# Layer 1's experts: 64 tokens gathered two experts per fetch, 192 dense, the last 64 with both coefficient halves in one stationary

## The chip, the cores and the metric

The kernel runs on one core of a Trainium2 chip. The metric is the device time of one execution in microseconds. A core has engines that run side by side, each with its own queue in order: TensorE (PE; the loads of its stationary operand are listed as PEld), VectorE (DVE), ScalarE (ACT), GpSimd (POOL), and SyncE (SP), whose queue here issues most transfers. Sixteen DMA engines move the data.

## The reference

Two layers, each a mixer and then an expert network (PEER) of 16,384 experts. Layer 0 runs the experts for 512 tokens (256 latent, 256 context), layer 1 for the 256 latent ones. For every token and each of eight heads a query is scored against two sets of 128 keys; the 16 best of each set are combined into 256 candidates, and the 16 best of those name experts.

```
s = einsum('thpd,hpkd->thpk', q, sub_keys)
sv, si = top_k(s, 16)
cand = sv[..., 0, :, None] + sv[..., 1, None, :]
cidx = si[..., 0, :, None] * 128 + si[..., 1, None, :]
best, pos = top_k(cand, 16)
eidx, gate = take_along_axis(cidx, pos), softmax(best)
ue, ve = take(u, eidx), take(v, eidx)          # rows of 1024
act = gelu(einsum('td,thkd->thk', x, ue)) * gate
ff = einsum('thk,thkd->td', act, ve)
```

So each token uses 128 of the experts, a row of u and one of v each.

## The kernel before

There are two ways to compute ff. **Dense:** all 16,384 experts are gone through in 128 blocks of 128, for all dense tokens at once: first half x times u, gelu, multiply by a matrix of gates (zero where an expert was not chosen), second half times v. **Gathered:** for 128 rows, an indirect DMA fetches for each row one chosen expert's u and v (8 KB); DVE takes the dot product with the row's token and adds v times the gated result. Layer 0 gathers for 128 tokens and is dense for 384; layer 1 is dense for all 256.

Float32 matmuls are split: an operand is written as a high part (`..h`, by ACT, rounded to float32r) and a low part (`..l`, the rest, by DVE or POOL), and `mm3` (lines 109 to 111) sums three float32r products.

Layer 1's expert network is `peer(1, ...)`, in these stages. *Choosing* (`evaluate`, `select`): PE makes a head's queries and scores, DVE the top 16. In between, `spare` computes the first half of some blocks ahead and puts them into DRAM (the stash): 32 of 128 blocks in layer 1, two of each eight. *Gates* (`dense`, lines 754 to 784): one-hot matmuls build the gate matrix G in units of 32 tokens; each unit is followed by two stashed blocks. `spare(len(waits))` computes those still missing. *The loop* (lines 922 on) runs over 128 blocks in an order written out by hand: each engine gets its instructions as the code lists them.

One pass of the loop, for block n: loads are issued (gates, v, u); PE makes the first half of block n+3 (24 matmuls, unless stashed) and ACT its gelu (`act`, line 735); for block n+1 DVE multiplies by the gates (line 903), ACT writes the high part `ch` (line 65), DVE the low part `cl` (line 73); for block n+5 ACT writes `uh` (line 719) and DVE `ul` (line 720), unless stashed; PE runs the second half of block n (`second`); for block n+2 ACT writes `vh` (line 880), DVE `vl` (line 881). In layer 0 a gather step follows, spread by `spent`: a piece of the next head's pick (DVE), `accum` for fetch e-3 (line 827, DVE), `fetch` e (line 811, POOL), `dot` for fetch e-2 (line 817, DVE), and on ACT a gelu and a scale of one column each (lines 818, 819).

Stashed blocks have no first half in the loop and no `uh` and `ul`. Raw u and v tiles come through a ring of five buffers. At the end the sums leave PSUM, are transposed and added to the stream (`combine`).

Of the kernel before, what the change touches and what calls it, by code (L numbers as in the profile page):

```python
# [9 lines left out]
F32 = mybir.dt.float32  # L10
F32R = mybir.dt.float32r
# [26 lines left out]
class Kern:  # L38
# [83 lines left out]
    def setup(self):  # L122
# [9 lines left out]
        make_identity(nc, self.ident)  # L132
        self.o1024 = c([128, 128])
# [362 lines left out]
    def peer(self, l, halves, gtile, nstash=0, nq=2, ng=(1, 1)):  # L496
# [3 lines left out]
        nt = 2 * len(halves)  # L500
        N = 128 * nt
        t0 = 1 if gtile else 0
        nd = nt - t0
        D0, ND = 128 * t0, 128 * nd
        with ExitStack() as st:
            m = self.open(st, f"p{l}")
            hh, hl = m([128, 8, N], F32R), m([128, 8, N], F32R)
            GA = m([128, nd, 128])
            IX = m([128, nd, 2, 128])
            iob = m([128, 16], BF16)  # L510
            nc.vector.tensor_copy(iob, self.iota[:, 0:16])
# [102 lines left out]
            with ExitStack() as st2:  # L614
# [8 lines left out]
                if gtile:  # L623
                    for g in range(2):
                        p = self.mm([128, 4, 128])
                        for k in range(4):
                            for n, x in enumerate((hh, hl)):
                                nc.tensor.matmul(p[:, k], x.bitcast(F32)[:, 4 * g + k, 0:128], self.ident, start=n == 0, stop=n == 1)
                        nc.scalar.activation(htok[:, g * 512:(g + 1) * 512].rearrange("p (k d) -> p k d", k=4), p, AF.Copy)
                keys = mq([128, 16, 128])  # L630
                nc.sync.dma_start(keys, i[f"keys{l}"])
                def evaluate(hd, w):

                    sv = mq([128, nd, 2, 16], F32, tag="sv", bufs=2)
                    si = mq([128, nd, 2, 16], U32, tag="si", bufs=2)
                    SC = []
                    for half in range(2):
# [8 lines left out]
                        sp = px([128, nt, 128], F32, tag="sp", bufs=2)  # L646
                        for t in range(nt):
                            nc.tensor.matmul(sp[:, t], qt[:, t * 128:(t + 1) * 128], keys[:, hp], start=True, stop=True)
                        sc = mq([128, nd, 128], F32, tag="sc", bufs=4)
                        nc.scalar.activation(sc, sp[:, t0:], AF.Copy)  # L650
                        if gtile:
                            nc.scalar.activation(scg[:, hp], sp[:, 0], AF.Copy)
                        SC.append(sc)
                    return hd, SC, sv, si

                def select(hd, SC, sv, si):
                    for half in range(2):
                        for t in range(nd):
                            topk(SC[half][:, t], sv[:, t, half], si[:, t, half], mq)
                    hs = slice(16 * hd, 16 * hd + 16)  # L660
                    choose(nd, sv, si, GA[:, :, hs], IX[:, :, :, hs], mq)

                with self.region():
                    prev = None
                    for b in range(4):
# [11 lines left out]
                    softmax(GA.rearrange("p t (h k) -> p (t h) k", k=16), 8 * nd, mq)  # L677
                    spare(nq)
            self.dense(l, t0, nd, hh[:, :, D0:], hl[:, :, D0:], IX, GA, first, stash, waits, spare, ng,
                       (htok, EI, gGA, scg, dacc, topk_parts, choose_parts, softmax) if gtile else None)  # L680

    def combine(self, l, tiles, halves, tmp, done=lambda k0: None):

        nc = self.nc
        for gq in range(2):
            for t, ff in tiles:
                hf = halves[t // 2]
                p = self.mm([128, 4, 128])
                for k in range(4):
                    nc.tensor.transpose(p[:, k], ff[:, (4 * gq + k) * 128:(4 * gq + k) * 128 + 128], self.ident)  # L690
                for k in range(4):
                    kk = 4 * gq + k
                    dst = self.s[hf][:, kk, (t % 2) * 128:(t % 2) * 128 + 128]
                    g = self.mt[l][:, 40 + kk, hf:hf + 1]
                    if k % 2:
                        x = tmp([128, 128], F32, tag="cmb", bufs=2)
# [43 lines left out]
    def dense(self, l, t0, nd, hh, hl, IX, GA, first, stash, waits, spare, ng, gather):  # L740
        nc, i = self.nc, self.i
        ND = 128 * nd
        halves = (0, 1) if l == 0 else (1,)
        with ExitStack() as st:
# [4 lines left out]
            with ExitStack() as st2:  # L749
                gb = self.open(st2, f"gb{l}")  # L750
                px = self.open(st2, f"gb{l}ps", space=PSUM)
                for t in range(nd):
                    tr = self.mm([128, 3, 128])
                    for n, x in enumerate((IX[:, t, 0], IX[:, t, 1], GA[:, t])):
                        nc.tensor.transpose(tr[:, n], x, self.ident)
                    trs = gb([128, 3, 128], F32, tag="trs", bufs=2)
                    nc.scalar.activation(trs, tr, AF.Copy)  # L757
                    for u in range(4):
# [473 lines left out]
```

## Time and profile before

| | us |
|---|---|
| runs: median of 3 | 2807.66 (2806.81 to 2807.99) |
| the profiled execution | 2807.95 |
| its span | 2806.2 |
| PE busy over the span | 2673.5 (95%) |
| DVE busy | 2028.2 (72%) |
| ACT busy | 1412.6 (50%) |
| POOL busy | 572.8 (20%) |

The span is what lies between the first and the last instruction of the program. PE's busy time is made of records whose ends are modelled and which overlap, so the rate of PE is read from starts. Start times below are microseconds from the span's start. A group by form keeps operand shapes apart.

### The profile page before, as it was taken

How to read it: one execution, taken by the hardware profiler on the slowest of the kernel's cores; microseconds unless marked ns; L12 is line 12 of the kernel's file. 1: busy time of each engine (PE TensorE's matmuls, PEld its weight loads, DVE VectorE, ACT ScalarE, POOL GpSimd, SP SyncE). 2: the span in 40 equal slices, each digit the busy share in tenths (PEclk: the TensorE clock that was granted, in tenths of full speed). 3: DMA queues.
4: the chain of work that ended last, by engine and by line, in shares of the span. 5: the costliest groups of instructions: out<-in, count | busy, mean ns of one | idle time of the engine just before them, and what ended most of it. 6: DMA issues, size and time to landing. Idle time of an engine off the chain costs nothing.

```text
span 2806.2 us, 40422 instructions
## 1 busy us (share of the span) xinstructions
PE 2673.5 (95%) x15043; PEld 2305.6 (82%) x15043; DVE 2028.2 (72%) x4323; ACT 1412.6 (50%) x2528; POOL 572.8 (20%) x538
## 2 busy tenths in 40 slices
PE   7999999999999999999999998998889999999998
PEld 4677778798988888898898896657789888888887
DVE  4688559999677787787878776656987655555555
ACT  5756543399444344444344436444388444444444
POOL 0000023288122222221222221005366000000000
PEclk9999999999999999999999999999999999999999
DMA  6334223445788878887778782354346665666653
GB/s 257 126 135 149 91 79 147 150 195 225 271 296 300 302 272 300 299 303 280 283 289 313 298 298 77 120 216 148 124 184 253 240 220 212 226 233 220 218 216 126
DMA packets 155204, 609.68 MB, mean 217 GB/s; under 512 B 10752, under 2 KB 90368, under 8 KB 90880
## 3 DMA queue, kind: packets, MB, share of 16 engines
q1 hardware_dynamic: 136576, 472.87, 46.0%
q0 software_dynamic: 18432, 134.23, 13.1%
q8 instruction: 119, 1.95, 0.3%
q14 instruction: 77, 0.63, 0.1%
HBM read 555.94 MB, written 51.12 MB: 216 GB/s over the span
## 4 chain that ended last, share of the span: by engine, by line
PE 47%; issue 22%; DVE 13%; POOL 12%; ACT 3%; DMA 1%; POOLq 0%; DVEq 0%; ACTq 0%
POOL uv L811 6%; POOL o L778 6%; PE t L109 6%; PE t L111 6%; PE t L110 6%; PE mm L111 5%; PE mm L109 5%; PE mm L110 5%; PE pj L111 2%; PE pj L109 2%; PE pj L110 2%; PE gp L780 2%; PE mm L168 1%; DVE eq L568 1%; PE pj L1065 1%
## 5 line engine op out<-in xcount | busy, mean ns | idle before, releaser
L109 PE MATMUL mm<-t,uh 128*128 128x384 f32 (+1 forms) x2048 | 637.1, 311 | 5.6 <-ACT c L735 3.0
L111 PE MATMUL mm<-t,ul 128*128 128x384 f32 (+1 forms) x2048 | 636.6, 311 | 2.2 <-POOL ul L720 2.2
L110 PE MATMUL mm<-t,uh 128*128 128x384 f32 (+1 forms) x2048 | 635.4, 310 | 0.1
L109 PE MATMUL t<-vh,ch 128*128 128x512 f32 x1280 | 502.4, 392 | 21.1 <-ACT ch L65 21.1
L111 PE MATMUL t<-vh,cl 128*128 128x512 f32 x1280 | 503.7, 394 | 0.0
L110 PE MATMUL t<-vl,ch 128*128 128x512 f32 x1280 | 501.6, 392 | 0.0
L109 PEld LDWEIGHTS mm<-t,uh 128*128 128x128 f32 x2048 | 387.0, 189 | 15.2 <-ACT c L735 3.7
L110 PEld LDWEIGHTS mm<-t,uh 128*128 128x128 f32 x2048 | 387.2, 189 | 9.2 <-DVE t L214 0.3
L111 PEld LDWEIGHTS mm<-t,ul 128*128 128x128 f32 x2048 | 387.2, 189 | 3.1 <-POOL ul L720 3.0
L720 DVE TENSOR_TENSOR ul<-r,uh 128x1024 fp32r<-128x1024 f32 x229 | 280.4, 1225 | 132.6 <-ACT uh L719 132.2
L811 POOL DMA_INDIRECT uv<-in_uv_dram,t x128 | 211.4, 1651 | 763.2 <-DVE t L827 715.8
L881 DVE TENSOR_TENSOR vl<-r,vh 128x1024 fp32r<-128x1024 f32 x256 | 312.6, 1221 | 73.3 <-PE t L110 51.0
L73 DVE TENSOR_TENSOR cl<-c,ch 128x384 fp32r<-128x384 f32 (+1 forms) x256 | 125.9, 492 | 308.0 <-ACT ch L65 308.0
L818 ACT ACTIVATE act<-act 128x1 f32<-128x1 f32 x128 | 26.0, 203 | 546.5 <-DVE uv L817 546.5
L109 PEld LDWEIGHTS t<-vh,ch 128*128 128x128 f32 x1280 | 241.4, 189 | 70.9 <-ACT ch L65 27.4
L719 ACT ACTIVATE uh<-r 128x1024 fp32r<-128x1024 f32 x256 | 270.4, 1056 | 52.3 <-PE mm L110 26.1
L111 PEld LDWEIGHTS t<-vh,cl 128*128 128x128 f32 x1280 | 241.0, 188 | 56.0 <-DVE cl L73 5.0
L110 PEld LDWEIGHTS t<-vl,ch 128*128 128x128 f32 x1280 | 240.9, 188 | 44.1
L880 ACT ACTIVATE vh<-r 128x1024 fp32r<-128x1024 f32 x256 | 268.8, 1050 | 0.0
L735 ACT ACTIVATE c<-mm 128x384 f32<-128x384 f32 (+1 forms) x256 | 110.7, 433 | 281.7 <-PE mm L111 280.4
L778 POOL TENSOR_SCALAR o<-t,trs 128x128 f32<-128x128 f32 x320 | 215.8, 693 | 52.8 <-ACT trs L757 45.8
L779 DVE TENSOR_SCALAR o<-t,trs 128x128 f32<-128x128 f32 x640 | 184.8, 362 | 0.0
(323 smaller groups left out, 4513.2 us busy)
## 6 DMA issues: line engine op xcount, KB each, us to landing
r<-in_ut_dram SPq DMA_DIRECT2D x128, 1024.0 KB
r<-in_vv_dram SPq DMA_DIRECT2D x128, 1024.0 KB
r<-in_wm_dram SPq DMA_DIRECT2D x48, 1024.0 KB
t<-buf SPq DMA_DIRECT2D x20, 2048.0 KB
gates<-t SPq DMA_DIRECT2D x32, 768.0 KB
r<-in_wq_dram SPq DMA_DIRECT2D x16, 1024.0 KB
gates<-t SPq DMA_DIRECT2D x16, 1024.0 KB
r<-in_ew_dram SPq DMA_DIRECT2D x14, 1024.0 KB
```

Source lines behind the costliest of these rows:

```text
L73: e[1].tensor_tensor(lo, x, hi.bitcast(F32), op=ALU.subtract)
L109: mm(p, a[0], b[0], start=first, stop=False)
L110: mm(p, a[0], b[1], start=False, stop=False)
L111: mm(p, a[1], b[0], start=False, stop=last)
L719: nc.scalar.activation(uh, t[:, x], AF.Copy)
L720: (eng or nc.vector).tensor_tensor(ul, t[:, x], uh.bitcast(F32), op=ALU.subtract)
L735: nc.scalar.activation(a, p, AF.Gelu_apprx_tanh)
L778: nc.gpsimd.tensor_scalar(o1, self.iota, trs[:, 0, tk:tk + 1], None, op0=ALU.is_equal)
L779: nc.vector.tensor_scalar(o2, self.iota, trs[:, 1, tk:tk + 1], trs[:, 2, tk:tk + 1], op0=ALU.is_equal, op1=ALU.mult)
L811: nc.gpsimd.indirect_dma_start(out=UV[e], out_offset=None, in_=i[f"uv{l}"], in_offset=bass.IndirectOffsetOnAxis(ap=EI[:, e:e + 1], axis=0))
L880: nc.scalar.activation(vh, v, AF.Copy)
L881: nc.vector.tensor_tensor(vl, v, vh.bitcast(F32), op=ALU.subtract)
```

## The change

In layer 1 the first 64 tokens go the gathered way. A fetch has 128 rows; row r and row r + 64 are the same token with different heads (0 to 3 and 4 to 7), so 64 fetches of two experts per token replace the dense work for these tokens. Their scores are put on both halves of the partitions (`scg`), their sums of both halves are added by a matmul with `halves` in `combine`. 192 tokens stay dense. The last 64 of these are scored the same way (`scb`: heads 0 to 3 in the upper half of the partitions, 4 to 7 in the lower), so heads 0 to 3 choose for one tile of 128 rows and heads 4 to 7 for two; the blocks of heads run in the order 0, 2, 1, 3. In the second half the high and low coefficients of these 64 tokens lie side by side in one stationary of 128 columns, against `vh` and `vl`: two matmuls for 64 tokens in place of three, and their pairs of rows are added by `pairs`. The coefficients are therefore stored as pairs (high, low), and the other tile's stationary is read with a step of two. The gate matrix has six units instead of eight. Layer 0 goes through the same code with its old sizes.

```diff
 def setup(self):
+        self.halves, self.pairs = c([128, 64]), c([128, 64])
+        nc.vector.tensor_add(self.halves, self.ident[:, 0:64], self.ident[:, 64:128])
+        nc.vector.tensor_add(self.pairs, self.ident[:, 0::2], self.ident[:, 1::2])
...
 def peer
+        ND = N - D0
+        nd, part64 = ND // 128, ND % 128 // 64
+        two = D0 == 64
+        W = 128 * nd + 64 * part64
+        NS = 64 if two else 128
...
+                for g in range(2):
+                    p = self.mm([128, 4, 128])
+                    for k in range(4):
+                        for o in (0, 64) if two else (0,):
                             for n, x in enumerate((hh, hl)):
+                                nc.tensor.matmul(p[o:o + D0, k], x.bitcast(F32)[:, 4 * g + k, 0:D0], self.ident, start=n == 0, stop=n == 1)
...
 def evaluate
+                        for t in range(nd):
+                            nc.tensor.matmul(sp[:, t], qt[:, D0 + t * 128:D0 + (t + 1) * 128], keys[:, hp], start=True, stop=True)
...
+                        rows, j = (slice(64 * (hd // 4), 64 * (hd // 4) + 64), hp % 8) if two else (slice(0, 128), hp)
+                        nc.tensor.matmul(sp[rows, 3], qt[:, 0:D0], keys[:, hp], start=True, stop=True)
+                        if two:
+                            nc.tensor.matmul(sp[rows, 2], qt[:, N - 64:N], keys[:, hp], start=True, stop=True)
+                            nc.scalar.activation(scb[rows, j], sp[rows, 2], AF.Copy)
+                        nc.scalar.activation(scg[rows, j], sp[rows, 3], AF.Copy)
+                        SC.append([sc[:, t] for t in range(nd)] + [scb[:, j] for _ in range(n - nd)])
...
-                    for b in range(4):
+                    for b in (0, 2, 1, 3) if two else range(4):
...
 def combine
+                    if rows is None:
+                        nc.tensor.transpose(p[:, k], x, self.ident)
+                    else:
+                        nc.tensor.matmul(p[:, k], x, rows, start=True, stop=True)
...
 def dense
-                for t in range(nd):
+                for t in range(nd + two):
+                    nk = min(128, ND - 128 * t)
...
-                    for u in range(4):
+                    for u in range(nk // 32):
...
-            if gather:
...
-                for e in range(131):
+            for e in range(NS + 3):
...
-            out = [[px([128, 512]) for _ in range(2)] for _ in range(nd)]
+            out = [[px([128, 512]) for _ in range(2)] for _ in range(nd + two)]
...
             def second(n, c, v):
+                if two:
+                    for x in range(2):
+                        xs = slice(x * 512, x * 512 + 512)
+                        mm = nc.tensor.matmul
+                        a, b = out[nd][x], c[:, 128:192].rearrange("p t y -> p (t y)")
+                        mm(a, b, v[0][:, xs], start=n == 0, stop=False)
+                        mm(a, b, v[1][:, xs], start=False, stop=n == 127)
+                    c = c[:, 0:128, 0], c[:, 0:128, 1]
+                    for x in range(2):
+                        xs = slice(x * 512, x * 512 + 512)
+                        self.mm3(out[0][x], c, (v[0][:, xs], v[1][:, xs]), n == 0, n == 127)
+                    return
...
             def gated(n):
+                    if two:
+                        S[n] = b2([128, ND, 2], F32R, tag="ch", bufs=2)
+                        self.split(c, S[n][:, :, 0], S[n][:, :, 1])
+                        return
...
-        self.peer(1, (1,), False, nstash=32, nq=6, ng=(2, 2))
+        self.peer(1, (1,), 64, nstash=32, nq=6, ng=(2, 2))
...
-    r["uv0"] = np.concatenate([d["p_u"][0], d["p_v"][0]], axis=1)
+    for l in range(2):
+        r[f"uv{l}"] = np.concatenate([d["p_u"][l], d["p_v"][l]], axis=1)
```

In the loop, DVE's queue before, two blocks (line 903 multiplies by the gates, 73 is the low part of the coefficients, 720 and 881 the low parts of u and v):

```order
L903 TENSOR_TENSOR c_21527<-c_21527,gates_21257 128x256
L73 TENSOR_TENSOR cl_21608<-c_21527,ch_21607 128x256
L720 TENSOR_TENSOR ul_21612<-r_21554,uh_21611 128x1024
L881 TENSOR_TENSOR vl_21628<-r_21448,vh_21627 128x1024
L903 TENSOR_TENSOR c_21581<-c_21581,gates_21257 128x256
L73 TENSOR_TENSOR cl_21639<-c_21581,ch_21638 128x256
L720 TENSOR_TENSOR ul_21643<-r_21554,uh_21642 128x1024
L881 TENSOR_TENSOR vl_21659<-r_21552,vh_21658 128x1024
L903 TENSOR_TENSOR c_21550<-c_21550,gates_21257 128x256
```

and after, two blocks (the same instructions at lines 945, 73, 744 and 911; 527 to 529 are a piece of a pick, 857 accumulates, 847 is the dot):

```order
L945 TENSOR_TENSOR c_20584<-c_20584,gates_20322 128x192
L73 TENSOR_TENSOR ch_20736<-c_20584,ch_20736 128x192
L744 TENSOR_TENSOR ul_20740<-r_20622,uh_20739 128x1024
L911 TENSOR_TENSOR vl_20754<-r_20620,vh_20753 128x1024
L527 MATCH_REPLACE s_20757<-sv_20527,t_16970 128x128
L528 MAX sv_20527<-s_20757 128x8
L529 MAX_INDEX si_20528<-sv_20527,s_20757 128x8
L857 SCALAR_TENSOR_TENSOR t_16971<-uv_20531,act_20651,t_16971 128x1024
L847 SCALAR_TENSOR_TENSOR uv_20612,act_20764<-uv_20612,t_16967 128x1024
L945 TENSOR_TENSOR c_20680<-c_20680,gates_20618 128x192
L73 TENSOR_TENSOR ch_20796<-c_20680,ch_20796 128x192
L744 TENSOR_TENSOR ul_20800<-r_20706,uh_20799 128x1024
```

Between a block's `vl` and the next block's multiply now stand a piece of a pick, an accumulate and a dot.

ACT's queue before, in the same loop (735 the gelu of the first half, 65 the high part, 719 and 880 the high parts of u and v):

```order
L880 ACTIVATE vh_21658<-r_21552 128x1024
L735 ACTIVATE c_21687<-mm_21662 128x256
L65 ACTIVATE ch_21690<-c_21550 128x256
L719 ACTIVATE uh_21694<-r_21635 128x1024
L880 ACTIVATE vh_21710<-r_21552 128x1024
L735 ACTIVATE c_21743<-mm_21718 128x256
```

and after (759, 65, 743 and 910 are these, 848 and 849 the gelu and the scale of a dot):

```order
L759 ACTIVATE c_21234<-mm_21209 128x192
L65 ACTIVATE ch_21237<-c_21134 128x192
L743 ACTIVATE uh_21240<-r_21107 128x1024
L910 ACTIVATE vh_21254<-r_21105 128x1024
L848 ACTIVATE act_21271<-act_21271 128x1
L849 ACTIVATE act_21271<-act_21271,t_16969 128x1
L759 ACTIVATE c_21300<-mm_21275 128x192
L65 ACTIVATE ch_21303<-c_21183 128x192
```

The two small instructions stand ahead of the next block's first-half gelu and high part.

PE's second half of a block before:

```order
L109 MATMUL t_20572<-vh_23262,ch_23294 128x512
L110 MATMUL t_20572<-vl_23263,ch_23294 128x512
L111 MATMUL t_20572<-vh_23262,cl_23295 128x512
L109 MATMUL t_20573<-vh_23262,ch_23294 128x512
L110 MATMUL t_20573<-vl_23263,ch_23294 128x512
L111 MATMUL t_20573<-vh_23262,cl_23295 128x512
L109 MATMUL t_20574<-vh_23262,ch_23294 128x512
L110 MATMUL t_20574<-vl_23263,ch_23294 128x512
L111 MATMUL t_20574<-vh_23262,cl_23295 128x512
L109 MATMUL t_20575<-vh_23262,ch_23294 128x512
L110 MATMUL t_20575<-vl_23263,ch_23294 128x512
L111 MATMUL t_20575<-vh_23262,cl_23295 128x512
```

and after (920 and 921 are the matmuls of the packed 64 tokens):

```order
L920 MATMUL t_20304<-vh_25343,ch_25375 128x512
L921 MATMUL t_20304<-vl_25344,ch_25375 128x512
L920 MATMUL t_20305<-vh_25343,ch_25375 128x512
L921 MATMUL t_20305<-vl_25344,ch_25375 128x512
L109 MATMUL t_20302<-vh_25343,ch_25375 128x512
L110 MATMUL t_20302<-vl_25344,ch_25375 128x512
L111 MATMUL t_20302<-vh_25343,ch_25375 128x512
L109 MATMUL t_20303<-vh_25343,ch_25375 128x512
L110 MATMUL t_20303<-vl_25344,ch_25375 128x512
L111 MATMUL t_20303<-vh_25343,ch_25375 128x512
```

Ten matmuls of 512 columns stand where twelve did.

## Rows read from the trace of the kernel before

**Rows 1.** Windows: us; busy PE, PEld, DVE, ACT, POOL; clock, DMA share, GB/s

```profile
717.00:1697.00 980.00, 960.11 (x4774) 860.54 (x4774) 760.65 (x1163) 401.04 (x740) 211.56 (x129) 1.00 0.79 291
1923.00:2046.00 123.00, 96.78 (x719) 93.16 (x719) 115.89 (x487) 44.52 (x72) 54.77 (x23) 0.89 0.37 131
2046.00:2165.00 119.00, 114.14 (x912) 110.68 (x912) 100.81 (x288) 109.20 (x226) 88.75 (x129) 0.98 0.58 220
2181.00:2797.00 616.00, 615.37 (x3758) 550.66 (x3756) 356.91 (x476) 288.43 (x440) 0.00 (x0) 1.00 0.59 214
```

**Rows 2.** Timeline, DVE, layer 1's loop: start, duration, instruction, idle before

```profile
2295.88 1.22 DVE L720 TENSOR_TENSOR ul<-r,uh 128x1024 fp32r<-128x1024 f32 x1 [0.53 <-ACT uh L719]
2297.03 1.22 DVE L881 TENSOR_TENSOR vl<-r,vh 128x1024 fp32r<-128x1024 f32 x1
2298.16 0.42 DVE L903 TENSOR_TENSOR c<-c,gates 128x256 f32<-128x256 f32 x1
2300.54 0.43 DVE L73 TENSOR_TENSOR cl<-c,ch 128x256 fp32r<-128x256 f32 x1 [1.96 <-ACT ch L65]
```

**Rows 3.** Timeline, ACT, the same stretch

```profile
2299.82 0.38 ACT L735 ACTIVATE c<-mm 128x256 f32<-128x256 f32 x1 [3.02 <-PE mm L111]
2300.10 0.41 ACT L65 ACTIVATE ch<-c 128x256 fp32r<-128x256 f32 x1
2300.40 1.05 ACT L719 ACTIVATE uh<-r 128x1024 fp32r<-128x1024 f32 x1
```

**Rows 4.** Timeline, PE, the same stretch

```profile
2302.16 0.39 PE L111 MATMUL t<-vh,cl 128*128 128x512 f32 x1
2302.39 0.28 PE L109 MATMUL mm<-t,uh 128*128 128x256 f32 x1
...
2305.22 0.40 PE L109 MATMUL t<-vh,ch 128*128 128x512 f32 x1
```

**Rows 5.** Timeline, PE, layer 1's mixer: passes of two columns

```profile
1876.20 0.95 PE L177 MATMUL mm<-t,modm 128*128 128x2 f32 x8
1877.01 0.36 PE L110 MATMUL pj<-l,whi 128*128 128x256 f32 x1
1877.21 0.28 PE L109 MATMUL pj<-h,whi 128*128 128x256 f32 x1
```

**Rows 6.** Timeline, DVE, layer 0's loop: accumulate and dot

```profile
1205.19 1.26 DVE L827 SCALAR_TENSOR_TENSOR t<-uv,act,t 128x1024 f32<-128x1024 f32 x1
1206.37 1.22 DVE L817 SCALAR_TENSOR_TENSOR uv<-uv,t 128x1024 f32<-128x1024 f32 x1
```

**Rows 7.** Timeline, ACT, layer 0's loop, behind that dot

```profile
1207.63 0.20 ACT L818 ACTIVATE act<-act 128x1 f32<-128x1 f32 x1 [4.42 <-DVE uv L817]
1207.87 0.29 ACT L819 ACTIVATE act<-act,t 128x1 f32<-128x1 f32 x1
1208.07 0.47 ACT L735 ACTIVATE c<-mm 128x384 f32<-128x384 f32 x1
1208.44 0.51 ACT L65 ACTIVATE ch<-c 128x384 fp32r<-128x384 f32 x1
1208.85 1.05 ACT L719 ACTIVATE uh<-r 128x1024 fp32r<-128x1024 f32 x1
```

**Rows 8.** Groups by form, DVE, the multiply by the gates

```profile
L903 DVE TENSOR_TENSOR c<-c,gates 128x384 f32<-128x384 f32 x128 | 71.0, 555 | 0.0
...
L903 DVE TENSOR_TENSOR c<-c,gates 128x256 f32<-128x256 f32 x128 | 53.6, 419 | 0.0
```

**Rows 9.** Timeline, ACT, stashed blocks with little else on the engines

```profile
2017.19 0.37 ACT L735 ACTIVATE c<-mm 128x256 f32<-128x256 f32 x1
...
2030.07 0.36 ACT L735 ACTIVATE c<-mm 128x256 f32<-128x256 f32 x1
```

**Rows 10.** The tile uv: an idle time of DVE before it, and landings

```profile
  DMA uv<-in_uv_dram,t: 0.5, 1
...
DMA to landing us min/median/max: 5.5/6.6/11.9
```

More of the change, by code (lines that the diff above doesn't have):

```diff
@@ L738, in first_half, with dense @@
         return load, part, dots, act, hold
-    def dense(self, l, t0, nd, hh, hl, IX, GA, first, stash, waits, spare, ng, gather):
+    def dense(self, l, D0, nd, ND, hh, hl, IX, GA, first, stash, waits, spare, ng, gather):
         nc, i = self.nc, self.i
-        ND = 128 * nd
+        two = ND > 128 * nd
         halves = (0, 1) if l == 0 else (1,)
@@ new lines, in dense, with pick @@
+            htok, EI, gGA, scg, dacc, topk_parts, choose_parts, softmax = gather
+            NS = EI.shape[1]
+            gp = self.open(st, f"gp{l}")
+            def pick(hd):
+                sv = gp([128, 1, 2, 16], F32, tag="sv", bufs=2)
+                si = gp([128, 1, 2, 16], U32, tag="si", bufs=2)
+                for half in range(2):
+                    yield from topk_parts(scg[:, 2 * hd + half], sv[:, 0, half], si[:, 0, half], gp)
+                    yield
+                hs = slice(16 * hd, 16 * hd + 16)
+                ix = gp([128, 1, 2, 16], F32, tag="ix", bufs=2)
+                yield from choose_parts(1, sv, si, gGA[:, None, hs], ix, gp)
+                yield
+                softmax(gGA[:, None, hs], 1, gp)
+                nc.vector.scalar_tensor_tensor(EI[:, hs], ix[:, 0, 0], 128.0, ix[:, 0, 1], op0=ALU.mult, op1=ALU.add)
@@ new lines, in accum, with advance @@
+            def accum(e):
+                x, a = UV.pop(e)[:, 1024:2048], ACT.pop(e)
+                if e == 0:
+                    nc.vector.tensor_scalar(dacc, x, a, None, op0=ALU.mult)
+                else:
+                    nc.vector.scalar_tensor_tensor(dacc, x, a, dacc, op0=ALU.mult, op1=ALU.add)
+            picks = [pick(0)]
+            def advance():
+                if picks and next(picks[0], True):
+                    picks.pop()
+            for _ in picks[0]:
+                pass
@@ new lines, in dense, with step @@
+            picks.clear()
+            for e in range(NS + 3):
+                def step(e=e):
+                    if e % 16 == 1 and e < NS - 16:
+                        picks.append(pick(e // 16 + 1))
+                    advance()
+                    if 3 <= e:
+                        accum(e - 3)
+                    if e < NS:
+                        fetch(e)
+                    if 2 <= e < NS + 2:
+                        dot(e - 2)
+                gsteps.append(step)
+            gsteps.append(lambda: self.combine(l, [(0, self.halves if two else None, dacc)], halves, b2))
@@ L934, in dense @@
             FF = []
[L935 to L936 removed]
+            for t in range(nd + two):
+                ff = b2([128, 1024], F32, tag="vh", bufs=3)
                 for x in range(2):
                     self.copy((nc.scalar, nc.vector)[x], ff[:, 512 * x:512 * x + 512], out[t][x])
[L939 removed]
+                FF.append((D0 + 128 * t, None if t < nd else self.pairs, ff))
             def done(k0):
```

160 lines of the change are left out of this document (60 added, 100 removed).

## The prediction

> **What bounds the kernel now.** I read the windows by stage first, then the timelines of one stage engine by engine. In layer 1's expert loop, 2181 to 2797 us, PE is busy 615 of 616 us, DVE 357 and ACT 288 [rows 1]: PE sets the pace. Its work repeats every eight expert blocks: six blocks compute their 24 first-half matmuls in the loop, two (the stashed ones) only load them, and all eight have 12 matmuls of 512 columns. A 512-column matmul holds PE for 0.23 us (2302.16 to 2302.39); 24 of 256 columns lie between 2302.39 and 2305.22, 0.118 each [rows 4]. So eight blocks take 6 x 24 x 0.118 + 8 x 12 x 0.230 = 39.1 us, and 16 such periods 625; the window shows 616, because the first blocks were prepared ahead (9 us).
>
> DVE has slack there only because nothing else is asked of it. It works in order, and stands before each `cl` until ACT has written `ch`, which stands behind the activation of a block that PE has just finished [rows 2, 3]. Layer 0 shows the loop with a gather step in every block: PE is busy 960 of 980 us, DVE 761, and the DMA engines 79% at 291 GB/s [rows 1].
>
> The stage ahead, choosing experts (1923 to 2046 us), is set by DVE: 115.9 of 123 us busy, PE 96.8. In the build of the gates (2046 to 2165) PE, ACT and DVE all stand between 101 and 114 of 119 [rows 1].
>
> **The change, part by part.** *Choosing.* Before: eight heads of two token tiles, 116 us of DVE, 14.5 a head. After: four heads of one tile and four of two, twelve tile-heads in place of sixteen. In proportion that is 29 us less; the short fixed instructions of each head stay, so 25. But PE's floor is near: its busy time here falls little, since the query matmuls stay, the stashed blocks are no faster (below), and a third score matmul and 32 token-transposing matmuls come in. It can't end much under 97 us of work. I take 20 less (10 to 26).
>
> *Gates.* Eight units of 32 tokens in 119 us are 14.9 each; the start and the change of tile stay, so I take 14 a unit and 28 less for two units (24 to 30). Each unit also carried two stashed blocks. Of the 32, eight plus six come in the choosing and twelve in six units: six are left to the end instead of two. Alone on the engines, with POOL making their low halves, four such blocks took 12.9 us [rows 9], so +13. The first pick of the gathered tokens (DVE) lies beside these on an engine that idles there: nothing, or 8 us if that cover fails.
>
> *First half at 192 columns.* No row has this form with under 256 columns. Its bounds: a pass with only two moving columns still took 0.111 us (eight of them and one 256-column matmul lie between 1876.20 and 1877.21, so (1.01 - 0.12) / 8) [rows 5], a 256-column one 0.118. So 0.111 to 0.118, and I take 0.116, near the wider row: what repeats is the load of the 128-column stationary, not the columns. 64 fewer columns give PE 24 x 0.002 = 0.05 us a block. What PE gains is two of twelve 512-column matmuls, 0.46 us a block: 6 x 24 x 0.116 + 8 x 10 x 0.230 = 35.1 us for eight blocks.
>
> The Trainium skill says otherwise ("TensorE: Matmul & The Clock Gate", section "Back-to-back issue gap"): at full clock one matmul follows another after N / 2.4 + 2.5 ns, which for 192 columns is an estimate of 82.5 ns. By it PE's eight blocks would be 30.3 us. The two-column row does not bear it out, where the stationary changes each time.
>
> *The gather in the loop.* 64 fetches come in, and with each on DVE one accumulate and one dot, on ACT two tiny activations, on POOL the fetch; the order shows them behind `vl` and ahead of the next block's multiply. All durations are in layer 0 [rows 6, 7]. The question is the chain DVE to ACT to DVE, so I walk it from one `vl` to the next:
> without a step: vl to multiply 1.13; the multiply 0.35 (0.42 at 256 and 0.56 at 384 columns give 0.35 at 192 [rows 8]); hand-over 0.03; `ch` to `uh` 0.25 (0.30 at 256 [rows 3], 0.41 at 384 [rows 7]); `uh` 1.05; hand-over 0.04; `ul` to `vl` 1.15 [rows 2]. Together 4.00 us. Without `uh` and `ul`, where the block five ahead is stashed, `vh` takes their place: 2.85.
> With a step: vl to accumulate 1.13, accumulate to dot 1.18, dot to gelu 1.26, gelu to scale 0.24, scale to activation 0.20 [rows 6, 7], activation to `ch` 0.24 (0.28 at 256, 0.37 at 384), then 0.25 + 1.05 + 0.04 + 1.15 as above: 6.74. A step costs 2.74, of which 0.4 is new standing: gelu and scale wait for the dot, and the `ch`, `uh` and `vh` of the whole block are queued behind them on ACT, and behind those DVE's `cl`, `ul`, `vl` and in time PE.
> Eight blocks without steps: 6 x 4.00 + 2 x 2.85 = 29.7, under PE's 35.1. But four steps fall in them: 29.7 + 4 x 2.74 = 40.7, over PE's 35.1 and over the 39.1 of before. **The loop changes its bound from PE to this chain.** 16 x 29.7 = 475, 64 x 2.74 = 175, three more picks at 9 (a tile-head is 7.2 by half of 14.5, and its softmax waits on ACT): 27. Less the 9 of the start as before: 668, against 616, +52. Low end: if DVE filled all its waits, PE would bound (rival one). High end: `ch` and `cl` now stand two apart in memory. The trace has no such row; nothing or, by the rise of the multiply from 256 to 384 columns (0.136), up to 0.2 us a block, 26 us. I take nothing, since the number of elements falls.
>
> *Small.* The token transposes fall in PE's wait for the first query weights; the gathered tokens' combine adds some 2 us at the end; layer 0 keeps its instructions and only reorders a few: nothing, or 2 us either way.
>
> **Sum**, on the profiled execution's 2807.95 us (2806.2 of span and 1.75 around it; the median of the runs is 2807.66, 0.3 less): - 20 - 28 + 13 + 52 + 2 = +19, so **2827 us**.
>
> **Rivals.** *One, faster: PE stays the bound of the loop.* It would if a gather step cost the chain under (35.1 - 29.7) / 4 = 1.35 us, half of my 2.74, by ACT and DVE working ahead far enough. Then 16 x 35.1 - 9 = 553, 63 under before: 2807.95 - 20 - 28 + 13 - 63 + 2 = 2712. For it: layer 0 has a step in each block and no stall of PE to speak of. Against: a block there has 24 x 384 and 18 x 512 columns to hide it, over 8 us. By the spacing that the Trainium skill gives ("TensorE: Matmul & The Clock Gate", above), and by it alone, this rival would end at an estimate of 2712 - 16 x 4.8 = 2635.
>
> *Two, slower: loads land late.* The loop would move about 200 MB (48 and 64 loads of 1 MB, 64 fetches of 1 MB, 13 MB of gates and 3 of stash) in 668 us, 300 GB/s, above layer 0's 291 at 79%. A `ut` tile is asked for when the ring buffer comes free and needed after about 7 us here, longer in layer 0. If half the 48 waited for one more load in the queue, 3.5 us, that is +84: 2911. Against it: a fetch landed after 5.5 to 11.9 us in layer 0 and DVE waited for one of them once, 0.5 us [rows 10].
> The Trainium skill has a rule that would make it worse ("SBUF — State Buffer", section "SBUF: two separate sides"): while DVE runs a two-port operation, GpSimd can't write the descriptors of its own DMAs. The landings and the one wait of [rows 10] speak against its weight beside this loop's DVE work, which is layer 0's.
>
> *Three: 192 columns in this number format stream slower*, say two passes' worth, 0.23 us. PE is then 6 x 24 x 0.23 + 18.4 = 51.5 us for eight blocks, 16 x 51.5 - 9 = 815, and the time 2974. Only the missing row speaks for it.
>
> *Four: the loop loses less than I say and the early stages win more* (-26, -30, +10, +40, +2): 2804, no change.
>
> **How the numbers follow.** Forecast 0.67, rival one 0.14, two 0.06, three 0.04, four 0.09. My forecast's own range is 2810 to 2855: the stage terms' ends and the spacing of stored halves. To leave 2 in 10 out at most I take 2795 to 2868, which holds the forecast, four and part of two. 0.2% (5.6 us) is about what a measurement of this kernel can tell from no change. Faster by more: rival one and a fifth of four, 0.16. Within: most of four (0.07) and a little of the forecast (0.02), 0.09. Slower: the rest of the forecast (0.65), two and three, 0.75.
>
> **What would show it.** The loop's window: PE idle some 100 us of 670 with `ch` (ACT) or `ul` (DVE) as releasers, DVE busy near three quarters; one `vl` to the next 4.0 without and 6.7 us with a step. First-half matmuls of 192 columns starting 0.111 to 0.118 apart; at 0.09 the stationary's load was not the floor. Choosing near 103 us, gates near 91, 19 instead of 6 us of stashed blocks behind them. I am wrong if PE stays busy without gaps in the loop, or if DVE stands before dots for the fetch.

## The result, and the profile after

The changed kernel takes 2869.68 us (median of 4 runs, 2867.06 to 2872.46) against 2807.23: 1.0223 times as long, interval 1.021 to 1.0237, some 62 us more. Forecast were 2827 and at most 2868. The direction was right; the loss was three times as large.

The profiled execution took 2867.06 us, 59.1 more than the one before. Windows of it by stage, columns as in [rows 1]: layer 0's loop, choosing, gates, the stretch behind the gates, layer 1's loop. As in [rows 1], the gates end with the gelu of the last unit's second stashed block (ACT's timeline has it at 2164.81 before and at 2146.81 after).

```profile
717.00:1697.00 980.00, 960.35 (x4777) 861.02 (x4776) 760.83 (x1162) 401.06 (x740) 211.41 (x128) 1.00 0.80 292
1923.00:2054.00 131.00, 106.10 (x791) 96.99 (x791) 104.92 (x390) 50.41 (x105) 56.05 (x23) 0.91 0.35 119
2054.00:2147.00 93.00, 84.79 (x708) 82.12 (x708) 83.08 (x255) 85.21 (x175) 68.27 (x96) 0.98 0.57 221
2147.00:2180.00 33.00, 28.44 (x216) 27.58 (x216) 8.88 (x10) 13.72 (x23) 14.79 (x8) 0.84 0.73 268
2180.00:2855.00 675.00, 590.14 (x3525) 515.10 (x3526) 514.36 (x795) 309.97 (x586) 105.03 (x69) 0.95 0.77 282
```

| us | before | after | change | forecast |
|---|---|---|---|---|
| choosing | 123 | 131 | +8 | -20 |
| gates | 119 | 93 | -26 | -28 |
| behind the gates | 16 | 33 | +17 | +13 |
| loop | 616 | 675 | +59 | +52 |
| end | 9 | 10 | +1 | +2 |

**The loop** went as forecast. One step on DVE, timeline of a stretch without `ul` (the block five ahead is stashed): accumulate, dot, multiply by the gates, `cl` (named ch here), `vl`, with idle time and releaser in brackets. It answers to [rows 2].

```profile
2275.95 1.28 DVE L857 SCALAR_TENSOR_TENSOR t<-uv,act,t 128x1024 f32<-128x1024 f32 x1
2277.15 1.22 DVE L847 SCALAR_TENSOR_TENSOR uv<-uv,t 128x1024 f32<-128x1024 f32 x1
...
2278.29 0.35 DVE L945 TENSOR_TENSOR c<-c,gates 128x192 f32<-128x192 f32 x1
2279.45 0.36 DVE L73 TENSOR_TENSOR ch<-c,ch 128x192 fp32r<-128x192 f32 x1 [0.80 <-ACT ch L65]
2280.39 1.23 DVE L911 TENSOR_TENSOR vl<-r,vh 128x1024 fp32r<-128x1024 f32 x1 [0.58 <-ACT vh L910]
```

The same on ACT, which answers to [rows 3, 7]: gelu and scale of the dot, then the block's activation, `ch` and `vh`.

```profile
2278.41 0.20 ACT L848 ACTIVATE act<-act 128x1 f32<-128x1 f32 x1 [4.23 <-DVE uv L847]
2278.65 0.29 ACT L849 ACTIVATE act<-act,t 128x1 f32<-128x1 f32 x1
2278.85 0.31 ACT L759 ACTIVATE c<-mm 128x192 f32<-128x192 f32 x1
2279.06 0.36 ACT L65 ACTIVATE ch<-c 128x192 fp32r<-128x192 f32 x1
2279.32 1.04 ACT L910 ACTIVATE vh<-r 128x1024 fp32r<-128x1024 f32 x1
```

ACT stands 4.23 us until the dot ends, and DVE then stands for `ch` and `vh`. From the `vl` before (2274.21) to this one are 6.18 us; the forecast's walk gives 2.85 + 2.74 and 0.60 for a piece of a pick, 6.19. A block without a step took 4.08 (`vl` at 2263.82 and 2267.90), forecast 4.00. What PE and DVE wait for over the loop (total, times, longest):

```profile
PE t L920 <- DVE ch L73: 83.8, 58, 4.0
DVE ch L73 <- ACT ch L65: 81.0, 128, 2.0
```

First-half matmuls of 192 columns in a busy stretch of PE; this answers to [rows 4, 5]:

```profile
2298.09 0.27 PE L109 MATMUL mm<-t,uh 128*128 128x192 f32 x1
...
2298.42 0.28 PE L109 MATMUL mm<-t,uh 128*128 128x192 f32 x1
```

Three lie in 0.33 us, 0.11 each, the two-column pass's floor. The 82.5 ns that the prediction took from the Trainium skill ("TensorE: Matmul & The Clock Gate", section "Back-to-back issue gap") don't hold for this stream; the section gives its formula for an isolated matmul, and says that it comes out too low where the columns are few.

**Ahead of the gates** the gain is gone. ACT's timeline there (`L581` is the softmax's exponential, `uh` and `c` stashed blocks, `trs` the gates' first copy):

```profile
2031.40 0.36 ACT L581 ACTIVATE t<-t 128x192 f32<-128x192 f32 x1 [16.10 <-DVE t L557]
2031.67 1.04 ACT L743 ACTIVATE uh<-r 128x1024 fp32r<-128x1024 f32 x1
...
2054.03 0.31 ACT L759 ACTIVATE c<-mm 128x192 f32<-128x192 f32 x1
2054.25 0.48 ACT L787 ACTIVATE trs<-mm 128x384 f32<-128x384 f32 x1
```

The exponential stands in ACT's order ahead of six stashed blocks. It waits for DVE's last head, and they wait behind it; in the kernel before it stood behind all of them but two gelus, and the gates started 1 us after DVE's end instead of 15.7 (2038.60 to 2054.25). Before, on ACT and DVE (`L576` is the exponential, `L580` DVE's last operation of the stage):

```profile
2041.20 0.42 ACT L576 ACTIVATE t<-t 128x256 f32<-128x256 f32 x1 [6.92 <-DVE t L552]
2045.29 0.42 DVE L580 TENSOR_TENSOR t<-t,sm 128x256 f32<-128x256 f32 x1
2046.64 0.49 ACT L757 ACTIVATE trs<-mm 128x384 f32<-128x384 f32 x1 [2.11 <-PE mm L755]
```

DVE's own end came 7 us earlier than before (2045.71, now 2038.60), not 20. Starts on DVE in the changed kernel (a head begins with `L523`; the last line is DVE's last operation of the stage):

```profile
2001.10 0.28 DVE L523 MAX8 sv<-sc 128x8 f32<-128x128 f32 x1
...
2010.44 0.28 DVE L523 MAX8 sv<-sc 128x8 f32<-128x128 f32 x1
...
2022.86 0.28 DVE L523 MAX8 sv<-sc 128x8 f32<-128x128 f32 x1
...
2037.32 1.28 DVE L585 TENSOR_TENSOR t<-t,sm 128x192 f32<-128x192 f32 x1
```

A head of one tile takes 9.3 us here, the next one, of two tiles, 12.4: half the tiles are three quarters of the time (1.5 of the 9.3 went to one small operation that stood beside one of GpSimd; DVE's `t<-best` at 2006.29 took 1.67 us instead of 0.15). After the first scores (8.1 us) the profile lists no wait of DVE in this stage, and the last head's scores were copied by 2014.00, 8.9 us before DVE took them.

Behind the gates GpSimd does the like: its first fetch waits for the first pick, with a `ul` of the trailing blocks queued behind.

```profile
2147.90 1.04 POOL L841 DMA_INDIRECT uv<-in_uv_dram,t  x1 [14.79 <-DVE t L585]
2148.97 2.35 POOL L744 TENSOR_TENSOR ul<-r,uh 128x1024 fp32r<-128x1024 f32 x1
```

### The profile page after: what moved, and what is told of

Its sections match the earlier page's. It is cut to its first block, busy times and chain, and to the rows that moved or that the text cites. A ratio compares the mean times of both kernels' runs of the same rounds, so it can differ in the third digit from the quotient of the medians.

```text
span 2865.3 us, 40167 instructions
## 1 busy us (share of the span) xinstructions
PE 2642.8 (92%) x14788; PEld 2257.2 (79%) x14788; DVE 2156.1 (75%) x4513; ACT 1420.9 (50%) x2658; POOL 668.7 (23%) x578
## 4 chain that ended last, share of the span: by engine, by line
PE 29%; issue 24%; DVE 23%; ACT 11%; POOL 10%; DMA 1%; POOLq 0%; ACTq 0%; DVEq 0%
POOL uv L841 6%; DVE vl L911 4%; POOL o L808 4%; ACT uh L743 3%; PE mm L111 3%; PE mm L110 3%; PE mm L109 3%; DVE t L857 3%; DVE uv L847 3%; PE gp L810 2%; ACT vh L910 2%; PE pj L111 2%; PE pj L109 2%; PE pj L110 2%; PE t L109 2%
## 5 line engine op out<-in xcount | busy, mean ns | idle before, releaser
L841 POOL DMA_INDIRECT uv<-in_uv_dram,t x192 | 316.6, 1649 | 1309.2 <-DVE t L857 1201.6
L109 PE MATMUL t<-vh,ch 128*128 128x512 f32 x1024 | 410.0, 400 | 20.2 <-ACT ch L65 20.2
L109 PEld LDWEIGHTS mm<-t,uh 128*128 128x128 f32 x2048 | 394.8, 193 | 35.1 <-ACT c L759 25.1
L110 PE MATMUL t<-vl,ch 128*128 128x512 f32 x1024 | 408.0, 398 | 0.0
L111 PE MATMUL t<-vh,cl 128*128 128x512 f32 x768 | 302.3, 394 | 0.0
L109 PEld LDWEIGHTS t<-vh,ch 128*128 128x128 f32 x1024 | 198.3, 194 | 63.9 <-ACT ch L65 26.3
L857 DVE SCALAR_TENSOR_TENSOR t<-uv,act,t 128x1024 f32<-128x1024 f32 x190 | 242.3, 1275 | 3.2 <-ACT act L849 3.2
L847 DVE SCALAR_TENSOR_TENSOR uv<-uv,t 128x1024 f32<-128x1024 f32 x192 | 233.9, 1218 | 0.4 <-DMA uv<-in_uv_dram,t 0.4
L110 PEld LDWEIGHTS t<-vl,ch 128*128 128x128 f32 x1024 | 198.1, 193 | 37.1
L744 POOL TENSOR_TENSOR ul<-r,uh 128x1024 fp32r<-128x1024 f32 x31 | 77.4, 2500 | 602.8 <-PE mm L192 365.9
L808 POOL TENSOR_SCALAR o<-t,trs 128x128 f32<-128x128 f32 x288 | 195.5, 700 | 34.0 <-ACT trs L787 34.0
L920 PE MATMUL t<-vh,ch 128*128 128x512 f32 x256 | 112.3, 439 | 84.0 <-DVE ch L73 83.8
```

The costliest lines, as they stand in the source:

```text
L109: mm(p, a[0], b[0], start=first, stop=False)
L110: mm(p, a[0], b[1], start=False, stop=False)
L111: mm(p, a[1], b[0], start=False, stop=last)
L744: (eng or nc.vector).tensor_tensor(ul, t[:, x], uh.bitcast(F32), op=ALU.subtract)
L808: nc.gpsimd.tensor_scalar(o1, self.iota, trs[:, 0, tk:tk + 1], None, op0=ALU.is_equal)
L841: nc.gpsimd.indirect_dma_start(out=UV[e], out_offset=None, in_=i[f"uv{l}"], in_offset=bass.IndirectOffsetOnAxis(ap=EI[:, e:e + 1], axis=0))
```

## The experiments

All start from the changed kernel. Executions of one kernel lie up to 9 us apart (x7: 2787.5 to 2796.3), and the profiles of x9, x11, x12 and x14 have gathered 7 to 8 us more by the end of layer 0; so stretches are compared from their own starts.

### The loop: chain, traffic or PE

**x3_short_steps**: in `dot` and `accum`

```
-   ... x[:, 0:1024], x[:, 0:1024], 1.0, htok ...; ... dacc, x, a, dacc
+   ... x[:, 0:16], x[:, 0:16], 1.0, htok[:, 0:16] ...; ... dacc[:, 0:16], x[:, 0:16], a, dacc[:, 0:16]
```

> Layer 1's dots and accumulates on VectorE work on 16 of their 1024 columns (the gathered tokens' sums are left out but for these); all 64 fetches, ACT's gelu and scale and the picks stay. Chain theory (the loop is set by the in-order chain VectorE - ACT - VectorE, of which a step is 2.7 us): the chain falls under PE's 35 us for eight blocks, PE becomes the bound, the loop takes 555 to 585 us instead of 675 and the kernel 2770 to 2785. Traffic theory (fetches and late loads hold the loop up): the loop stays within 20 us of 675, the kernel above 2845.

**x4_three_fetches**: in `fetch` (and `dot` writes its products to a tile of its own)

```
+                if two and e >= 3:
+                    UV[e] = KEEP[e % 3]
+                    return
```

> Layer 1 fetches only the first three of its 64 pairs of expert rows; the other steps' dots and accumulates work at full width on those three tiles (products go to a tile of their own), so the gathered tokens' sum is another one. Chain theory: nothing changes in the order of VectorE and ACT, the loop stays within 8 us of 675 and the kernel within 10 us of 2869. Traffic theory (64 fetches of 1 MB beside the loads): the loop falls by 60 us or more, the kernel to 2810 or less.

**x8_unpacked**: in `second`

```
-   mm(a, b, v[0][:, xs], ...); mm(a, b, v[1][:, xs], ...)     # b: c[:, 128:192] with both halves
+   self.mm3(out[nd][x][0:64], (c[:, 128:192, 0], c[:, 128:192, 1]), (v[0][:, xs], v[1][:, xs]), ...)
```

The sums then need no `pairs` at the end.

> The part of the change that puts the last 64 tokens' high and low coefficients in one stationary is undone: high and low are two stationaries of 64 columns, so PE does two more 512-column matmuls in each of 128 blocks, 59 us of PE at 0.23. Chain theory (PE has slack in the changed loop): eight blocks come to 38.8 us of PE, still under the chain's 43; within 12 us of 2869. Rival (PE sets the loop's pace): 2869 + 59 = 2928.

Measured: x3 2755.09 us (0.9813 of before, 0.9794 to 0.9833), x4 2865.74 (1.0208, 1.0187 to 1.0228), x8 2874.97 (1.024, 1.0219 to 1.026). The loop's window in x3:

```profile
2181.00:2744.00 563.00, 552.31 (x3524) 494.23 (x3524) 381.31 (x795) 312.79 (x586) 60.08 (x69) 1.00 0.88 339
```

in x4:

```profile
2180.00:2855.00 675.00, 589.53 (x3528) 514.42 (x3528) 514.82 (x796) 309.63 (x585) 3.09 (x9) 0.96 0.52 188
```

and in x8:

```profile
2183.00:2860.00 677.00, 627.81 (x3782) 514.78 (x3781) 514.64 (x796) 310.33 (x584) 105.51 (x70) 0.98 0.77 282
```

The periods, from one eighth multiply by the gates to the next, in us:

| kernel | second to ninth period |
|---|---|
| before | 39.1 each |
| after | 42.8 43.7 43.4 43.4 43.0 45.9 41.8 46.3 |
| x4 | 42.8 43.7 43.4 43.4 43.0 45.9 41.8 46.3 |
| x8 | 42.9 43.7 43.4 43.4 43.0 45.9 41.9 46.3 |
| x3 | 34.4 35.7 34.9 35.0 34.6 39.0 36.0 35.8 |
| x7 | 36.7 40.8 37.2 37.5 37.2 41.4 36.5 39.3 |

Taking away a third of the traffic (188 instead of 282 GB/s), or giving PE 256 matmuls more, leaves the periods where they were; taking away most of DVE's work in a step brings them near the 35.1 forecast for PE, at 339 GB/s, and the kernel lower than expected. Traffic and PE are out; DVE's queue sets the loop.

**x9_gelu_later**: gelu and scale are collected and issued behind the next block's `part`.

```
                     if n + 5 < 128 and n + 5 not in late:
                         P[n + 5] = part(n + 5)
+                    flush()
```

> The changed kernel, but in layer 1's loop each dot's gelu and scale stand on ACT behind the next block's activation, ch and uh instead of ahead of them; VectorE's order stays. Chain theory: the 0.4 us that ACT's queue stands at a dot leaves the chain in each of 64 steps: 20 to 28 us less, 2842 to 2850. Rival (VectorE's accumulate and dot alone make the step's cost): within 6 us of 2869.

Measured 2871.94 (1.0222, 1.0205 to 1.0239): no gain, the rival. ACT in that kernel, a `uh`, the gelu and scale moved behind it, and `vh`:

```profile
2297.04 1.04 ACT L743 ACTIVATE uh<-r 128x1024 fp32r<-128x1024 f32 x1
2297.98 0.19 ACT L856 ACTIVATE act<-act 128x1 f32<-128x1 f32 x1
2298.20 0.29 ACT L857 ACTIVATE act<-act,t 128x1 f32<-128x1 f32 x1
2298.40 1.04 ACT L921 ACTIVATE vh<-r 128x1024 fp32r<-128x1024 f32 x1
```

`vh` now starts 0.42 us later, and DVE stands for it before `vl`. Over the 64 steps DVE's way from the multiply to `cl` is 18 us shorter than in the changed kernel, and its way on to `vl` 19 us longer. The wait was moved, not removed.

**x7_loop_order**: the loop's body is written out anew, here in short words, with what fills each wait of DVE.

```
+   mul c(n+1); ACT: ch(n+1), vh(n+2)
+   step: accum(e - 3), fetch(e)            # while ch is made
+   cl(n+1); vl(n+2)
+   ACT: act(n+3), uh(n+5)
+   dot(e - 2)                              # while uh is made; its gelu and scale follow uh
+   ul(n+5); second(n)
```

> The changed kernel with the order of layer 1's loop alone changed, same instructions: VectorE's accumulate stands between the gate multiply and cl (which waits for ACT's ch), its dot between vl and ul (which waits for ACT's uh); ACT makes ch and vh ahead of the next activation, and a dot's gelu and scale behind uh. Chain theory: VectorE fills its waits with the step, some 5.3 us of work a block with a step and 3.0 without, 33 us for eight blocks against PE's 35.1; the loop falls from 675 to between 560 and 600, the kernel to 2755 to 2795. Rival (VectorE's sum of work or the DMA engines, 77% busy in a loop of 675 us, set it): the loop stays above 630, the kernel above 2825.

Measured 2789.07 (0.9941, 0.9925 to 0.9958), 81 us less than the changed kernel. Its loop:

```profile
2180.00:2776.00 596.00, 566.71 (x3526) 500.61 (x3527) 507.59 (x796) 315.57 (x586) 115.74 (x70) 0.99 0.84 320
```

DVE does the same work (508 us of 596 instead of 514 of 675) and stands 88 us instead of 161; PE is busy 95%.

**x10_order_unpacked**: x7 with the edit of x8 in `second`.

> x7_loop_order with high and low coefficients of the last 64 tokens in two stationaries again, two more 512-column matmuls a block, 59 us of PE. In the changed kernel the same edit cost 5 us. If x7's loop (PE busy 567 of 596 us) is bound by PE, it costs here what is over the slack of 29 us: 25 to 50 us more than x7's 2789, near 2825. If the chain still sets it: within 12 us of 2789.

Measured 2808.83 (1.0005, 0.9995 to 1.0016): 20 us over x7, where the same edit cost 5 in the changed kernel, within the spread there. Less than the 25 to 50 expected; that neither engine binds this loop all the time would explain it, but wasn't tested apart.

### Ahead of the gates

**x1_choose_exp**: in `softmax`, `self.tc.keep_in_program_order(x)` on the exponential, and in `peer`

```
+                    if l == 1:
+                        spare(nq)
                     softmax(GA.rearrange("p (h k) -> p h k", k=16), W // 16, mq)
```

> The choosing stage's softmax exponential is put behind the activations of the six stashed blocks in ACT's order (instead of ahead of their first u part); nothing else changes. Order theory (the early stages' gain was lost because ACT stands at that exponential until VectorE has chosen the last head, 16 us, with the six stashed blocks queued behind it): those blocks run while VectorE still chooses, the first gate transpose copy starts near 2040 us instead of 2054, and the whole kernel takes 10 to 19 us less, near 2855. Rival (the choosing is paced by PE and by GpSimd beside VectorE, and the stashed blocks cost PE the same wherever they stand): under 4 us less.

Measured 2857.39 (1.0179, 1.0162 to 1.0196), 12 less. ACT there:

```profile
2037.44 0.36 ACT L581 ACTIVATE t<-t 128x192 f32<-128x192 f32 x1 [3.74 <-DVE t L557]
...
2042.88 0.49 ACT L792 ACTIVATE trs<-mm 128x384 f32<-128x384 f32 x1 [2.49 <-PE mm L787]
```

The gates start 11.4 us earlier, still only 3.8 before the 2046.64 of the kernel before.

**x6_no_stash_in_heads** and **x13_heads_alone**: x1 with

```
-                            spare(1)
+                            spare(1 if l == 0 else 0)
-        self.peer(1, (1,), 64, nstash=32, nq=6, ng=(2, 2))
+        self.peer(1, (1,), 64, nstash=32, nq=14, ng=(2, 2))     # x6
+        self.peer(1, (1,), 64, nstash=24, nq=6, ng=(2, 2))      # x13
```

> As x1_choose_exp, and the eight stashed blocks that stand one behind each head's queries are put behind the last head instead (14 there instead of 6). Theory (PE paces the choosing: a head every 11.6 us, of which the stashed block is 2.7, and only then VectorE's last two heads, of two tiles and 12.4 us each): the heads' queries come every 9 us, VectorE's last head ends 8 to 14 us earlier, the gates start near 2032 and the kernel takes 8 to 12 us less than x1_choose_exp, 2845 to 2850, if PE gets its 14 blocks done beside VectorE. Rival (VectorE paces it): VectorE ends at the same time as before or up to 4 us earlier, and the kernel is within 4 us of 2857, or slower where the 14 blocks run over.

> As x1_choose_exp, but the eight stashed blocks that stand behind the heads are not stashed at all (24 stashed blocks: six behind the last head, twelve beside the gates, six after them); eight more blocks compute their first half in the loop. Theory (PE gives the choosing its pace, a head every 11.6 us of which 2.7 are a stashed block, and VectorE only ends two two-tile heads after PE's last): the heads come every 9 us, VectorE's last head ends near 2025 as in x6_no_stash_in_heads, the six blocks fit beside it, and the gates start near 2030, 11 to 15 us before x1's; the loop gives back 8 x 1.15 = 9 us in the chain, so the kernel is 2 to 6 us under x1's 2857. Rival (VectorE's selection work sets the pace): the gates start within 4 us of x1's 2043 and the kernel is 5 to 9 us slower than x1.

x6: 2859.25 (1.0185, 1.0168 to 1.0202), as x1: DVE's last head ends at 2026 us instead of 2041, but the 14 blocks run to 2045. x13: 2851.21 (1.0155, 1.0138 to 1.0172), 6 less than x1. ACT of x13, the exponential and the gates' first copy:

```profile
2018.97 0.36 ACT L581 ACTIVATE t<-t 128x192 f32<-128x192 f32 x1 [1.02 <-DVE t L557]
...
2024.38 0.49 ACT L792 ACTIVATE trs<-mm 128x384 f32<-128x384 f32 x1 [2.46 <-PE mm L787]
```

The gates start 18.5 us before x1's and 22 before those of the kernel before: the forecast's 20, but with eight blocks less in the stage. DVE's choosing, from the first `L523` to the end of the last head, took 90.9 us instead of x1's 112.6 with as many operations, and 95.0 in x6; the profiles list no wait of DVE for scores beyond the 8 us at the start. So the blocks between the heads lengthened DVE's own work. Operations over 0.3 us longer than the shortest of their kind add up to 27 us in x1 and 21 in x13; the rest is DVE's order, in which x13 has operations of two heads by turns, and how much each is worth wasn't tested apart. The loop, from first to last multiply, grew by 13 us for eight blocks (9 expected).

### Behind the gates

**x2_both_exp** is x1 with the first pick's exponential kept in program order too; **x5_trail_vector** is x1 with the first edit below; **x11_26_stashed** is the changed kernel with the second.

```
-            spare(len(waits))
+            spare(len(waits), nc.vector if two else nc.gpsimd)
-        self.peer(1, (1,), 64, nstash=32, nq=6, ng=(2, 2))
+        self.peer(1, (1,), 64, nstash=26, nq=6, ng=(2, 2))
```

> As x1_choose_exp, and the first pick's exponential too is put behind the activations of the stashed blocks that are left after the gates. Order theory: ACT no longer stands some 4 us there and the trailing blocks and their GpSimd parts don't queue behind it; 5 to 10 us less than x1_choose_exp, so 15 to 29 us under the changed kernel, near 2847. Rival (the 41 us behind the gates are the six blocks' own work on GpSimd and PE): within 3 us of x1_choose_exp.

> As x1_choose_exp, and the low halves of the u parts of the stashed blocks left behind the gates are made by VectorE instead of GpSimd. Theory: in x2_both_exp GpSimd stood 14.8 us at the first fetch, which waits for the first pick on VectorE, with the low halves of those blocks queued behind it; with the halves on VectorE (1.15 us each instead of 2.4) the blocks go at PE's 2.7 us and the loop starts 8 to 14 us earlier than in x1_choose_exp: 2843 to 2850. Rival (the loads, 290 GB/s at 75% there, or the pick's own VectorE work hold that stretch up): within 4 us of x1_choose_exp's 2857.

> The changed kernel with 26 stashed blocks instead of 32, so that none is left behind the gates; six more blocks compute their first half in the loop. Theory (the 41 us between the gates and the loop are six stashed blocks, GpSimd's stand at the first fetch, and the pick's exponential): that stretch falls to 16 to 20 us, and in the chain-bound loop six blocks cost 1.15 us each in place: 14 to 20 us less, 2850 to 2856. Rival (the first pick alone holds the stretch up): the stretch stays above 30 us and the kernel is within 6 us of 2869 or slower.

x2: 2861.51 (1.0197, 1.018 to 1.0214), no gain over x1. GpSimd still stood at the first fetch, by its timeline:

```profile
2137.90 1.04 POOL L849 DMA_INDIRECT uv<-in_uv_dram,t  x1 [14.83 <-DVE t L843]
```

x5: 2857.20 (1.0178, 1.0161 to 1.0195), no gain that the time shows; in its profile the stretch from the gates' last copy on ACT to the loop's first multiply is 37 us instead of x1's 42. x11: 2858.97 (1.0176, 1.0159 to 1.0193), 11 less, where 14 to 20 were expected. This stretch is 21.6 us instead of the changed kernel's 42.1, its loop from first to last multiply 675.1 instead of 667.5, about the 7 expected for six blocks in the chain. So the six blocks cost 20 there, 3.4 each. In the same stretch stand two more blocks, those of the last unit; without them 15 are left, in x11 as in the changed kernel. The kernel before had 20.8 with four blocks of 3.2 in it, 8 without. The 7 us more are what is new there, the first pick and what waits for it.

### Together

**x12_together**: x7, x1 and x5. **x14_together_26**: x12 with `nstash=26`.

> The three edits that the earlier runs point to together: the loop's order of x7_loop_order, the choosing's exponential of x1_choose_exp, VectorE's low halves for the trailing blocks of x5_trail_vector. If their gains add up: 2789 - 12 - 3 = 2774 (2768 to 2780), 1.2% under the kernel before. Rival (the loop starts earlier but waits for its loads, DMA 90% busy at 343 GB/s in x7's loop): 2782 to 2790.

> x12_together with 26 stashed blocks, none left behind the gates. The stretch before the loop should shorten by 16 to 20 us as in x11_26_stashed; the loop, near PE's bound now, takes six more first halves of 2.75 us on PE, 16.5 us: within 5 us of x12's 2779. If the loop hides them (PE was busy 567 of 596 us): up to 15 us less.

x12: 2779.47 (0.9893, 0.9876 to 0.9909). x14: 2771.61 (0.987, 0.9853 to 0.9886), 36 us under the kernel before and 98 under the changed one. In x14 the six blocks cost the loop 7 us, not 16.5: part of PE's slack hid them.

## Why the prediction was right or wrong

**Choosing, -20, was +8: the step that failed, 28 us.** It scaled DVE's 116 us by tile-heads, twelve for sixteen "in proportion", and let the gates start when DVE ends. Neither held. First, DVE ended 7 us earlier, 13 short of the 20: a head of one tile took 9.3 us against 12.4 for two tiles, not half. What is in such a head was not measured apart; that the stashed blocks between the heads lengthen it is shown by x6 and x13, why only in part. PE, whose last scores came as late as before, is not what held DVE at the end, since they lay ready for 8.9 us. Secondly, the gates started 15.7 us behind DVE's end instead of 0.9, another 15: the exponential stands ahead of six blocks on ACT. The code lists it there in both kernels; a scheduler, which orders this stage, had put it behind them in the kernel before, and not in this one. x1 moved it and got 11.4 of the 15, with DVE's end 4 us later. The forecast walked the new queue orders in the loop alone, not in this stage.

**Behind the gates, +13, was +17.** Six blocks at 3.4 us (forecast 3.2) were right. Of "nothing, or 8 us if that cover fails" for the first pick the second came, 7 us, part of them in the gates' window: the cover, an idle DVE, was there, but the pick's result is waited for by GpSimd, with the blocks' `ul` behind that wait, and by ACT's exponential. x2 and x5 don't settle how the 7 divide between GpSimd, ACT's exponential and the pick's own length.

**Gates, -28, was -26**: as taken, within the 24 to 30 given.

**Loop, +52, was +59: mechanism right, size nearly.** The change of bound from PE to DVE's chain is shown by x3, x4 and x8. Eight blocks were forecast at 40.7 and a share of the picks, 42.4; the fourteen periods of the profile's loop average 43.0. The "0.4 of new standing" behind gelu and scale is there, 0.24 a step from the multiply to `cl` (1.10 us instead of 0.86 on average), but moving gelu and scale gained nothing (x9). Rivals two (late loads, by x4) and three (192 columns slower, by the starts of 0.11) are out; of four, a smaller loss in the loop and larger gains ahead of it, nothing came. Rival one, PE as the bound, is what x7 nearly reaches by the order alone.

## What to carry to other kernels

An engine that is 58% busy beside a full one (DVE in the loop before) has no 42% to give if it works in order and its idle time is hand-overs: walk the chain for one block with the new work in it, then place the new instructions in the waits, which was worth 81 us here with nothing removed. For a stage ahead of the loop, don't scale a busy sum: read from the rows what one unit of the new size takes, and read in every in-order queue what stands behind an instruction that waits for another engine. Where a scheduler sets that order, read its order anew after each change.

## What the runs showed of the hardware

PE's clock. After PE had stood 3.58 us for `ch`, ten matmuls of the second half (timeline of PE, pairs of starts):

```profile
2279.87 0.50 PE L920 MATMUL t<-vh,ch 128*128 128x512 f32 x1 [3.58 <-DVE ch L73]
...
2281.35 0.63 PE L109 MATMUL t<-vh,ch 128*128 128x512 f32 x1
2281.78 0.63 PE L110 MATMUL t<-vl,ch 128*128 128x512 f32 x1
...
2283.85 0.39 PE L920 MATMUL t<-vh,ch 128*128 128x512 f32 x1
2284.08 0.40 PE L921 MATMUL t<-vl,ch 128*128 128x512 f32 x1
```

Windows of the stand, of the slow matmuls and of those behind, the clock third from the end:

```profile
2276.10:2279.80 3.70, 0.19 (x1) 0.00 (x0) 2.90 (x5) 1.36 (x5) 1.68 (x1) 1.00 1.04 367
2280.50:2283.40 2.90, 2.90 (x8) 2.34 (x7) 1.82 (x4) 1.42 (x3) 0.00 (x0) 0.50 1.02 423
2283.90:2286.00 2.10, 2.10 (x11) 1.73 (x10) 2.10 (x3) 0.34 (x1) 0.00 (x0) 1.00 1.00 421
```

The granted clock fell to 0.50 (1.2 GHz) behind the stand, with starts 0.43 apart, and came back with 0.23. This stand so cost PE 1.65 us more than its length (ten matmuls in 3.98 us instead of 2.33). In the chain-bound loop most of that is hidden (ACT stands 10.3 us of it all for PE's first half), and PE's 590 us busy hold some of it: x3, at clock 1.00, needs 552 for the same work.

GpSimd and VectorE. On GpSimd's timeline, the low halves of query weights:

```profile
1962.76 7.07 POOL L73 TENSOR_TENSOR wlo<-r,whi 128x1024 fp32r<-128x1024 f32 x3 [1.12 <-ACT whi L65]
```

On DVE's, two small operations of `choose` beside them, and the same two later with GpSimd idle:

```profile
1963.06 2.13 DVE L543 TENSOR_TENSOR cand<-sv 128x16 f32<-128x16 f32 x1
1965.12 2.42 DVE L569 CAST sif<-si 128x64 bf16<-128x64 uint32 x1
...
2016.12 0.16 DVE L543 TENSOR_TENSOR cand<-sv 128x16 f32<-128x16 f32 x1
2016.24 0.20 DVE L569 CAST sif<-si 128x64 bf16<-128x64 uint32 x1
```

Each small operation stood for one whole GpSimd operation of 2.4 us. The Trainium skill has this as an exclusive lock on a port pair that the two share ("SBUF — State Buffer", section "SBUF: two separate sides"), and these rows agree. In x1, where GpSimd's halves of the stashed blocks run beside DVE's last two heads, the last one ended 4 us later than in the changed kernel (2041.4 against 2037.4). The rows bear this out: from 2010 on, operations of DVE there stood 6.4 us in all over the shortest of their kind, each beside one of GpSimd, against 1.9 in the changed kernel.
